# Block 2's mixers, emitted step by step between the K steps of its products

## The chip, the cores and the metric

One core of a Trainium2 chip runs the whole program in one launch. The metric is the device time of one execution in microseconds (us). The kernel before was timed three times.

## The reference

A sequence of 1024 tokens of width 1024 (float32) goes through two blocks of two layers each. Block 1 (`first_block`) is not touched by the change. A layer of block 2 (`second_block`) does, for the 1024 tokens `x` and, in its first layer only, for 256 context tokens as well:

```
hx = rmsnorm(x, g_pre_mix) * (1 + sc1) + sh1
q, k, v, u, gv, f = split(hx @ w_in)                  # 512, 128, 128, 256, 256, 256 columns
attn = latent_window_attention(rope(q), rope(k), v, ck, cv, sink)   # 8 heads, blocks of 128
sgu  = spatial_gating(gelu(u), gelu(gv), w_sgu, b_sgu, g_sgu)
four = fourier_mix(f)                                 # real part of a 2D FFT over tokens x 64
y = concat(rmsnorm(attn), rmsnorm(sgu), rmsnorm(four)) @ w_out
x = x + g1 * rmsnorm(y)
x = x + g2 * rmsnorm(square(relu(norm2(x) @ w_ff1)) @ w_ff2)        # inner width 4096
```

Attention of a block of 128 tokens sees the block before, itself and the block after, and the 256 context tokens (`ck`, `cv`); so a score row has 512 or 640 entries. The vectors sc1, sh1, g1 and so on come from two conditioning vectors times `w_ada`.

## The kernel before, in words

Tokens lie in eight blocks of 128 partitions, worked on in two groups of four (`GT` = 4). Every large product is done in a split form: each factor is a high and a low fp32r part, and an output takes three matmuls a K step (high x high, high x low, low x high).

`product` (line 463 and on) is the loop that all stages share. For each of its K steps it loads a weight tile of 128 x 512 (`wr`, SP's queue), splits it (`split_weights`: ACT makes `wh` at line 202, DVE makes `wl` at line 203; with gains the lines are 439 and 440), and issues three matmuls for each of up to four outputs (lines 502 and 506, banks `mm`). After each K step it calls `self.tick()`, which runs one step of the first generator in the list `self.bg`. Block 1 puts its mixers (attention, retention, gated linear attention) into this list as generators. Block 2 of the kernel before puts nothing there: its mixers are plain functions, and each is emitted as a whole between two products.

What stands first in the program need not run first. When the program is built, a planner fixes the order of the instructions on each engine: it plays the program through with durations that it estimates, and whenever an engine comes free it takes, of the instructions whose inputs and buffers are then ready, the one that was emitted first. `high_priority(n)` makes an instruction count as emitted n instructions earlier: weight splits 3000 (`HP`), evictions, `norm_T` and `merge` 800 (`HE`), `norm_x` 600 (`HX`). On the chip each engine keeps the order that the planner fixed. Buffers go by tags with a set number of places: PSUM has four `mm`, one `mt`, two `sm`, one `o`; SBUF among others four `x`, sixteen `H`, five `uv`, five `Z`, eight `pt`.

The parts of block 2:

- `norm_x` and `norm_T`: for four blocks `x`, sum of squares (ACT line 375), reciprocal root (POOL lines 208, 209), scaling in place (DVE line 377), then for each of eight K tiles four transposes into `mt` (PE line 398), scale and shift, split. `norm_T(lazy=True)` makes each K tile only when it is asked for.
- `s2_attn` (one block of tokens): `queries` for a pair of heads (POOL copy `qd` line 1357, PE transposes, ACT `qh` line 1361, DVE `qh` line 1362); `scores` of a head (PE line 1373 into `sm`, DVE lines 1375 and 1380, ACT exp line 1381); `values` of the head before (PE transposes line 524, ACT and DVE copies `pT` lines 1394 and 1392, PE line 1398 into `o`); a closing normalization.
- `s2_sgu`: four matmuls (line 1291) and DVE lines. `features` and `s2_four`: the Fourier transform; `four_out` does four matmuls (line 1328) into `sm`, then `section` (ACT sum of squares, POOL root), DVE scaling (line 1333), two transposes (line 524), for eight outputs, and `s2_four_ctx` for two more.
- `merge`: for each of six K tiles four transposes into `mt` (line 1432) and a split into `H` tiles; two more K tiles are split from the Fourier output. `merge_out` is the product with `w_out`, whose eviction `residual` adds the old `x`, and stores the new one (POOL's queue, line 579).
- `ff`: eight rounds, each a product of 8 K steps, an eviction (ACT line 1463, DVE line 1464, split), and two products of 4 K steps. `mix1`, merge and `merge_out` of the second group, is called in the last round of the first group's `ff`. `mods_acc` computes the next layer's conditioning vectors between the rounds.

In layer 1 block 2 starts with attention of blocks 0 to 2, and the products of the context follow; then the context's mixers, block 3, group 1's products, the context's merge, `s2_four`, group 0's merge, `norm_T`, the queries of group 1, attention of blocks 4 to 7, and `ff`. Layer 2 is the same without the context, and its `merge_out` of group 0 uses `product_rows` (line 462), which finishes one output after the other.

Of the kernel before, what the change touches and what calls it, by code (L numbers as in the profile page):

```python
# [162 lines left out]
class Net:  # L163
# [106 lines left out]
    def mods_acc(self, w, vecs, bias, mds, width, chunks):  # L270
# [6 lines left out]
        def close(ch, acc, nv):  # L277
# [986 lines left out]
    def features(self, f):  # L1264
# [3 lines left out]
        Z = []  # L1268
# [7 lines left out]
        return Z  # L1276
# [8 lines left out]
    def s2_sgu(self, l, ug):  # L1285
# [3 lines left out]
        for h in range(4):  # L1289
# [3 lines left out]
            nc.vector.scalar_tensor_tensor(uv, ps, bs[:, h:h + 1], uv, ALU.add, ALU.mult)  # L1293
        for t in range(nt):
# [3 lines left out]
    def s2_four(self, Z):  # L1298
# [9 lines left out]
        V.tensor_sub(A, A, Z2)  # L1308
        c, s = 0, 1
# [4 lines left out]
        f4 = [self.T("uv", [P, 2, 512]) for _ in range(2)]  # L1314
        for r, W in ((0, Z3), (2, A), (1, Z2), (3, Z0)):
            ft = self.T("x", [P, 2, 2, 256])
            self.load(ft, self.a["ftab"][r].rearrange("p (a b c) -> p a b c", a=2, b=2))
            for mt in range(2):
                self.four_out(ft, W, mt, f4[mt].rearrange("p k (m r) -> p k m r", r=4)[:, :, :, r])
        return f4  # L1320

    def four_out(self, ft, W, mt, dst):
        nc = self.nc
        ps = self.T("sm", [P, 256])
        n = 0
        for nt_ in range(2):
            for cs in range(2):
                nc.tensor.matmul(ps, lhsT=ft[:, nt_, cs, mt * P:(mt + 1) * P], rhs=W[:, nt_, cs, :],  # L1328
                                 start=n == 0, stop=n == 3)
                n += 1  # L1330
        rr = self.section(ps, 256, 1.0 / 256, EPS)
        y = self.T("sc", [P, 256])
        nc.vector.tensor_scalar(y, ps, rr, None, ALU.mult)
        self.transposes(dst, y, 2)

    def s2_four_ctx(self, Z):
        ft = self.T("x", [P, 2, 2, 256])
        self.load(ft, self.a["ftab"][4].rearrange("p (a b c) -> p a b c", a=2, b=2))
        f4 = self.T("uv", [P, 2, 256])
        for mt in range(2):  # L1340
            self.four_out(ft, Z[0], mt, f4[:, :, mt * P:(mt + 1) * P])
        return f4

    def s2_attn(self, l, q, parts):
# [3 lines left out]
        O = self.T("o", [P, 512])  # L1348
        m8 = self.T("ti", [P, 8])
        m8b = self.T("ti", [P, 8])  # L1350
        den = self.T("ti", [P, 8])
        nk = sum(n for (_, n, _, _) in parts)
        scs = {}

        def queries(c):
            d = self.T("qd", [P, 2, 2, 64])
            nc.gpsimd.tensor_copy(d, q[:, c * P:(c + 1) * P].rearrange("p (h d) -> p h d", d=64).unsqueeze(2)
                                  .to_broadcast([P, 2, 2, 64]))
            ps = self.transposes(None, d.rearrange("p h c d -> p (h c d)"), 2)
# [3 lines left out]
            return hi, lo  # L1363

        def scores(h, hl):
# [3 lines left out]
            for i, (K, n, mask, _) in enumerate(parts):  # L1369
                w = n * P  # L1370
# [11 lines left out]
            scs[h] = sc  # L1382

        def values(h):
            sl = slice(h // 4 * 64, h // 4 * 64 + 64)
            sc = scs.pop(h)
            pT = self.T("pT", [P, 5, P])
            for c0 in range(0, nk, 4):
                n = min(4, nk - c0)
                tp = self.transposes(None, sc[:, c0 * P:(c0 + n) * P], n)  # L1390
                if c0:
                    nc.vector.tensor_copy(pT[:, c0:c0 + n, :], tp)
                else:
                    nc.scalar.copy(pT[:, c0:c0 + n, :], tp)  # L1394
            i = 0
            for (_, n, _, Vs) in parts:
                for j in range(n):
# [4 lines left out]
        hl = queries(0)  # L1402
        for h in range(9):
            if h < 8:
                scores(h, hl)
            if h % 2 and h < 7:
                hl = queries(h // 2 + 1)
            if h:
                values(h - 1)
        es = self.T("ti", [P, 8])  # L1410
        nc.vector.tensor_tensor(es, sk, m8, ALU.subtract)
        nc.scalar.activation(es, es, AF.Exp)
        nc.vector.tensor_add(den, den, es)
        nc.vector.reciprocal(den, den)
        a = self.T("qa", [P, 512])
        nc.vector.tensor_tensor(a.rearrange("p (h d) -> p h d", d=64), O.rearrange("p (h d) -> p h d", d=64),
                                den.unsqueeze(2).to_broadcast([P, 8, 64]), ALU.mult)
        r = self.section(a, 512, 1.0 / 512, EPS)
        nc.vector.tensor_scalar(a, a, r, None, ALU.mult)
        return a  # L1420

    def merge(self, at, u2, f4):
# [4 lines left out]
        with self.tc.high_priority(self.HE):  # L1427
            for k in range(6):
# [5 lines left out]
            for k in (6, 7):  # L1434
                self.split(*get(k), f4[:, k - 6, :])
        return get, nt
# [77 lines left out]
    def block2(self, cur, n_layers, out, early=None, rest=None):  # L1514
        nc, a = self.nc, self.a
        with ExitStack() as ctx:
            self.open(ctx, "b2", {"uv": 5, "Z": 5, "k2": 1, "sc": 1, "p5": 2, "pT": 2, "ck2": 1, "qd": 1, "qh": 3, "tr": 1},
                      {"ac": "x", "aw": "x", "row": "x", "L": "M", "qa": "pt", "ys": "pt"})
# [13 lines left out]
            for l in range(n_layers):  # L1532
# [15 lines left out]
                def attn(tb, q):  # L1548
                    lo, hi = max(0, tb - 1), min(NB - 1, tb + 1)
                    n = hi - lo + 1  # L1550
                    m0 = (lo - tb + 1) * P
                    at[tb] = self.s2_attn(l, q, [(K[:, :, lo * P:(hi + 1) * P], n, band[:, m0:m0 + n * P],
                                                  lambda j: V[:, lo + j, :]), cpart])

                x1, x2 = self.stream(), self.stream()
                if last:
                    x2 = out
                if l == 0:
# [8 lines left out]
                    if rest:  # L1567
                        kept = rest(lambda: self.project(l, 512, 768, "A", hx, self.e2_kv(0, cK, cV, False)))
                        h1 = self.norm_T(self.norm_x(kept), first(mx, l))
# [3 lines left out]
                if l or not rest:  # L1573
                    self.project(l, 512, 768, "A", hx, self.e2_kv(0, cK, cV, False))
                if l == 0:
                    for tb in range(3):
                        attn(tb, q0[tb])
                        if tb == 0:
                            self.project(l, 768, 1280, "A", h0, ev)
                if not last:  # L1580
                    self.project(l, 0, 512, "A", hx, self.e2_q(0, False, qc))
                    self.project(l, 768, 1280, "A", hx, self.e2_ug(2, ugc))
                    self.project(l, 1280, 1536, "B", hx, self.e2_f(2, fc))
                if l == 0:
                    self.project(l, 1280, 1536, "B", h0, self.e2_f(GT, f0))
                    Z = self.features(f0)
                    self.s2_sgu(l, ug0)
# [142 lines left out]
```

## Time and profile before

| | us |
|---|---|
| median of three runs | 3931.77 |
| lowest and highest | 3928.83 and 3936.1 |
| the profiled execution | 3937.08 |
| its span | 3935.3 |
| TensorE's mean granted clock in it | 0.986 of full |

| engine | busy us | share of the span |
|---|---|---|
| PE (matmul) | 3726.1 | 95% |
| PEld (weight load) | 3045.4 | 77% |
| DVE | 2445.6 | 62% |
| ACT | 1685.8 | 43% |
| POOL | 649.3 | 17% |

PE, PEld, DVE, ACT, POOL are TensorE's matmuls, its weight loads (which overlap the matmuls), VectorE, ScalarE and GpSimd; SP is the engine that issues the loads. A busy PE counts from a matmul's start to its modelled end, so overlapping matmuls count once. "A <- B" after an idle time says that A's engine stood until B's instruction was done. In the trace the parts lie so: block 1 from 0 to about 1240 us; block 2, layer 1: mixers about 1240 to 1840, `ff` of group 0 to 2140 with `mix1` at its end, `ff` of group 1 and the context to 2760; layer 2: mixers about 2680 to 3220, `ff` of group 0 to 3600 with `mix1` from about 3470, `ff` of group 1 to the end.

### The profile page before, as it was taken

Reading aid. Unit: us, or ns where it says so; the run is one execution under the profiler, and the core shown is the slowest. Engines: PE = TensorE matmul, PEld = TensorE weight load, DVE = VectorE, ACT = ScalarE, POOL = GpSimd, SP = SyncE. Lnnn points to the kernel's source line nnn. Section 1 sums busy time; section 2 is a strip of 40 time slices with the busy share of each in tenths; the row PEclk is TensorE's granted clock in tenths of the full one; section 3 lists DMA queues with packets and bytes.
Section 4 is the critical chain, followed back from the end, with each engine's and each line's share of the span. In section 5 each row is a group of like instructions: output and inputs, shape, how many; then the busy total and the mean of one; then the engine's idle time right before and its main releaser. Section 6 shows DMA issues by size and latency. Waiting matters only on the chain. (4 is left out here: it accounts for less than half of the span.)

```text
span 3935.3 us, 55613 instructions
## 1 busy us (share of the span) xinstructions
PE 3726.1 (95%) x19144; PEld 3045.4 (77%) x19144; DVE 2445.6 (62%) x5209; ACT 1685.8 (43%) x3652; POOL 649.3 (17%) x1026
## 2 busy tenths in 40 slices
PE   7999999999999898899999999999899999999998
PEld 6877777877877787677887788888777788887886
DVE  7686787687687657576545643335765654455444
ACT  4443444454454555464334422224554543344333
POOL 2021134243252212131001000000311100001000
PEclk9999999999999999999999999999999999999999
DMA  6144344343343313333333632222412123334332
GB/s 213 50 134 121 113 143 121 109 129 110 105 136 98 103 56 107 108 108 105 126 102 110 209 110 68 62 66 89 145 54 86 69 64 97 97 100 166 97 97 94
DMA packets 249453, 420.37 MB, mean 107 GB/s; under 512 B 32002, under 2 KB 101203, under 8 KB 249171
## 3 DMA queue, kind: packets, MB, share of 16 engines
q1 hardware_dynamic: 241426, 389.52, 32.0%
q0 software_dynamic: 7744, 27.30, 1.9%
q8 instruction: 151, 2.47, 0.3%
q14 instruction: 132, 1.07, 0.1%
HBM read 389.42 MB, written 27.30 MB: 106 GB/s over the span
## 5 line engine op out<-in xcount | busy, mean ns | idle before, releaser
L203 DVE TENSOR_TENSOR wl<-wr,wh 128x512 fp32r<-128x512 f32 (+2 forms) x948 | 644.2, 682 | 812.9 <-ACT wh L202 809.4
L202 ACT CAST wh<-wr 128x512 fp32r<-128x512 f32 (+2 forms) x948 | 553.7, 585 | 1208.8 <-PE mm L502 489.8
L502 PE MATMUL mm<-wh,M 128*128 128x512 f32 (+1 forms) x2944 | 945.9, 393 | 24.6 <-ACT M L202 14.8
L502 PE MATMUL mm<-wh,H 128*128 128x512 f32 (+2 forms) x2432 | 791.5, 396 | 12.3 <-DVE pe L654 3.6
L506 PE MATMUL mm<-H,wh 128*128 128x512 f32 x2240 | 727.4, 395 | 1.8 <-ACT wh L202 1.7
L502 PEld LDWEIGHTS mm<-wh,M 128*128 128x128 f32 x2944 | 550.0, 190 | 142.8 <-ACT M L202 23.1
L502 PE MATMUL mm<-wl,M 128*128 128x512 f32 (+1 forms) x1472 | 576.0, 391 | 0.4 <-DVE wl L203 0.4
L502 PEld LDWEIGHTS mm<-wh,H 128*128 128x128 f32 x2432 | 450.0, 192 | 100.5 <-issue 4.7
L506 PEld LDWEIGHTS mm<-H,wh 128*128 128x128 f32 x2240 | 418.8, 189 | 82.2 <-ACT wh L202 2.0
L502 PE MATMUL mm<-wl,H 128*128 128x512 f32 (+2 forms) x1216 | 471.1, 388 | 0.0
L506 PE MATMUL mm<-H,wl 128*128 128x512 f32 x1120 | 444.5, 397 | 0.0
L502 PEld LDWEIGHTS mm<-wl,M 128*128 128x128 f32 x1472 | 279.8, 190 | 49.2 <-DVE wl L203 1.2
L502 PEld LDWEIGHTS mm<-wl,H 128*128 128x128 f32 x1216 | 234.0, 192 | 35.1 <-issue 0.2
L506 PEld LDWEIGHTS mm<-H,wl 128*128 128x128 f32 x1120 | 212.2, 189 | 37.2
L1398 PEld LDWEIGHTS o<-kv,pT 128*128 128x128 f32 x1280 | 158.1, 192 | 25.0 <-ACT pT L1394 20.4
L317 POOL TENSOR_TENSOR ac<-ac,aw 128x256 f32<-128x256 f32 x168 | 142.9, 851 | 162.8 <-ACT aw L316 143.9
L1398 PE MATMUL o<-kv,pT 128*128 128x64 f32 x1280 | 167.5, 274 | 1.6 <-ACT pT L1394 0.9
L311 DVE SCALAR_TENSOR_TENSOR ac<-aw,c,ac 128x256 f32<-128x256 f32 x280 | 160.1, 572 | 5.9 <-DMA aw<-in_w_ada 3.1
L1483 DVE TENSOR_TENSOR Z<-Z,mm 128x512 f32<-128x512 f32 x224 | 140.2, 681 | 2.8 <-PE mm L502 2.5
L558 POOL TENSOR_TENSOR tm<-tm 128x1 f32<-128x1 f32 x34 | 6.6, 196 | 763.3 <-ACT pe L553 762.9
L1375 DVE CUSTOM_DVE_ANT_0 p<-sm,c,c 128x384 f32<-128x384 f32 (+1 forms) x144 | 82.2, 571 | 76.0 <-PE sm L1373 74.5
L1381 ACT ACTIVATE p<-p,ti 128x640 f32<-128x640 f32 (+2 forms) x144 | 110.8, 770 | 43.1 <-DVE ti L1380 39.7
(353 smaller groups left out, 5703.1 us busy)
## 6 DMA issues: line engine op xcount, KB each, us to landing
wr<-in_w_ff SPq DMA_DIRECT2D x512, 256.0 KB, 2.7
wr<-in_w_in SPq DMA_DIRECT2D x240, 256.0 KB, 2.7
wr<-in_w_out SPq DMA_DIRECT2D x144, 256.0 KB, 2.7
x<-xd SPq DMA_DIRECT2D x64, 512.0 KB, 4.9
aw<-in_w_ada SPq DMA_DIRECT2D x192, 128.0 KB, 2.1
x<-in_w_ada SPq DMA_DIRECT2D x96, 256.0 KB, 2.9
xd<-x POOLq DMA_DIRECT2D x44, 512.0 KB, 3.8
wr<-in_w_in SPq DMA_DIRECT2D x152, 128.0 KB, 2.1
```

The source lines that it names most:

```text
L202: self.nc.scalar.copy(hi, src)
L203: self.nc.vector.tensor_sub(lo, src, hi.bitcast(F32))
L311: nc.vector.scalar_tensor_tensor(acc[:, 0], wt, c[0], acc[:, 0], ALU.mult, ALU.add)
L317: nc.gpsimd.tensor_tensor(acc[:, 1], acc[:, 1], wt, ALU.add)
L502: nc.tensor.matmul(acc[j][:, :ncol], lhsT=x[:, j * P:(j + 1) * P], rhs=y[:, :ncol], start=first, stop=last)
L506: nc.tensor.matmul(acc[j][:m, :w], lhsT=y[:, j * P:j * P + m], rhs=x[:, :w], start=first, stop=last)
L558: nc.gpsimd.tensor_tensor(ss[j][:, 0:1], ss[j][:, 0:1], ss[j][:, 1:2], ALU.add)
L1375: nc.vector.tensor_tensor_reduce(sc[:, at:at + w], ps[:, :w], mask, 1.0, prev, ALU.add, ALU.max, accum_out=acc)
L1381: nc.scalar.activation(sc[:, :at], sc[:, :at], AF.Exp, bias=nm, accum_out=den[:, h:h + 1])
L1398: nc.tensor.matmul(O[:, h * 64:h * 64 + 64], lhsT=pT[:, i, :], rhs=Vs(j)[:, sl], start=i == 0, stop=i == nk - 1)
L1483: nc.vector.tensor_add(y, y, ps)
```

## The change

The mixers of block 2 become generators with a `yield` after each step, and are put on `self.bg`, so that `tick` emits one step after each K step of the products. In `s2_attn` one generator now does several blocks in a row; a step is one head's scores, the values of the head before, the transposes for the pair of heads that comes next, and the POOL copy for the pair after that. `four_out` becomes `four_outs`: the transposes of an output are emitted one step later, after the next output's matmuls, and the output is first copied out of PSUM by ACT. `norm_steps` emits one K tile of `norm_T` a step. `merge` loses its `high_priority`. `until(g)` ticks until g is done, `drain()` until the list is empty. The accumulators `ac` of `mods_acc` lie in `uv` places in block 2, not in `x` places, and their transposes go to `mt`, not to `o`. Layer 2's `merge_out` of group 0 uses `product` like the others, and attention of blocks 4 to 7 is on the list during it and during the `norm_T` that follows; in layer 1 it is on the list during `ff`. Some stages change places, as the diff of `block2` shows.

```
-                    ps = self.T("o", [P, each, nb, P])
+                    ps = self.T("mt", [P, each, nb, P])
...
+    def until(self, work):
+        while work in self.bg:
+            self.tick()
...
+    def four_outs(self, outs):
+        ft, have, pend = None, None, None
+        for r, W, mt, dst in outs + [(None,) * 4]:
+            y = None
+            if W is not None:
...
+                for n in range(4):
+                    nc.tensor.matmul(ps, lhsT=ft[:, n // 2, n % 2, mt * P:(mt + 1) * P], rhs=W[:, n // 2, n % 2, :],
+                                     start=n == 0, stop=n == 3)
+                y = self.T("pe", [P, 512])[:, :256]
+                nc.scalar.copy(y, ps)
+                rr = self.section(y, 256, 1.0 / 256, EPS)
+                nc.vector.tensor_scalar(y, y, rr, None, ALU.mult)
+            if pend:
+                self.transposes(pend[1], pend[0], 2)
+            pend = (y, dst)
+            yield True
...
+        units = [(n, h) for n in range(len(jobs)) for h in range(8)]
+        copies(0, 0)
+        yield True
+        queries(0, 0)
+        for i in range(len(units) + 1):
+            if i < len(units):
+                scores(*units[i])
+            if i:
+                n, h = units[i - 1]
+                values(n, h)
+                if h == 7:
+                    close(n)
+            if i + 2 < len(units):
+                (n, h), two = units[i + 1], units[i + 2]
+                if h % 2 == 0:
+                    queries(n, h // 2)
+                if two[1] % 2 == 0:
+                    copies(two[0], two[1] // 2)
+            yield True
...
-        with self.tc.high_priority(self.HE):
-            for k in range(6):
+        for k in range(8):
+            if k < 6:
                 ps = self.T("mt", [P, nt, P])
...
+                yield True
...
+    def norm_steps(self, xs, ab, room, keep):
+        ready, nt = self.norm_T(xs, ab, room=room, lazy=True)
+        keep += [ready, nt]
+        for k in range(8):
+            ready(k)
+            yield True
...
-                      {"ac": "x", "aw": "x", "row": "x", "L": "M", "qa": "pt", "ys": "pt"})
+                      {"ac": "uv", "aw": "x", "row": "x", "L": "M", "qa": "pt", "ys": "pt"})
...
+                    bg.append(attn((0,), q0))
+                    made = self.norm_steps(self.norm_x(kept), first(mx, l), "L", h1)
+                    bg += [made, attn((1, 2), q0[1:])]
+                    self.project(l, 768, 1280, "A", h0, ev)
+                    self.project(l, 0, 512, "A", hx, self.e2_q(0, False, qc))
+                    self.project(l, 768, 1280, "A", hx, self.e2_ug(2, ugc))
+                    self.project(l, 1280, 1536, "B", hx, self.e2_f(2, fc))
+                    bg.append(self.s2_sgu(l, ug0))
+                    bg.append(self.s2_attn(l, [(qc[t], [cpart], lambda a, t=t: atc.__setitem__(t, a)) for t in range(2)]))
+                    self.project(l, 1280, 1536, "B", h0, self.e2_f(GT, f0))
+                    bg.append(self.s2_features(fc, Zc))
+                    bg.append(self.s2_sgu(l, ugc))
                 else:
...
+                    made = self.norm_steps(self.norm_x(cur[4:8]), first(mx, l), "L", h1)
+                    bg += [attn((0, 1, 2), q0), made, self.s2_sgu(l, ug0)]
+                    self.project(l, 1280, 1536, "B", h0, self.e2_f(GT, f0))
+                bg.append(self.s2_features(f0, Z))
+                self.until(made)
+                self.project(l, 512, 768, "A", h1, self.e2_kv(4, K, V, True))
+                bg.append(attn((3,), q0[3:]))
+                self.project(l, 1280, 1536, "B", h1, self.e2_f(GT, f1))
+                bg.append(self.s2_features(f1, Z))
                 if not last:
+                    bg.append(self.s2_four_ctx(Zc, f4c))
                 self.project(l, 768, 1280, "A", h1, self.e2_ug(GT, ug1))
                 if not last:
...
+                    self.drain()
+                    for _ in self.merge(atc, ugc[0], f4c[0], mTc):
+                        pass
+                    bg.append(self.s2_four(Z, f4))
+                    self.merge_out(l, mTc, self.row_of(mc, 16), hc, c1)
+                    bg.append(self.s2_sgu(l, ug1))
+                    self.drain()
+                else:
+                    bg.append(self.s2_four(Z, f4))
+                    bg.append(self.s2_sgu(l, ug1))
+                    self.project(l, 0, 512, "A", h1, self.e2_q(4, True, q1))
+                    self.drain()
+                for _ in self.merge(at[:4], ug0[0], f4[0], mT0):
+                    pass
                 if last:
+                    bg.append(attn(range(4, 8), q1))
+                kept = self.merge_out(l, mT0, self.row_of(mx, 16, "Z"), cur[0:4], x1[0:4])
+                abf = second(mx, l)
+                if last:
+                    ready = self.norm_T(self.norm_x(kept), abf, room="H", lazy=True)
+                    for k in range(8):
+                        ready[0](k)
+                        for _ in range(2):
+                            self.tick()
+                    hT = ready
+                else:
+                    bg.append(self.norm_steps(self.norm_x(kept), abf, "H", hT))
                     self.project(l, 0, 512, "A", h1, self.e2_q(4, True, q1))
+                    self.drain()
+                    bg.append(attn(range(4, 8), q1))
...
                 def mix1():
-                    mT = self.merge(at[4:], ug1[0], f4[1])
+                    self.drain()
+                    for _ in self.merge(at[4:], ug1[0], f4[1], mT1):
+                        pass
```

## Rows read from the trace of the kernel before

**Rows 1.** The page's first part: busy us (share of the span) xinstructions.

```profile
PE 3726.1 (95%) x19144; PEld 3045.4 (77%) x19144; DVE 2445.6 (62%) x5209; ACT 1685.8 (43%) x3652; POOL 649.3 (17%) x1026
```

**Rows 2.** Windows: length, busy PE PEld DVE ACT POOL (instructions), PEclk, DMA share, GB/s.

```profile
100.00:1240.00 1140.00, 1077.33 (x5782) 870.55 (x5780) 880.65 (x1956) 530.32 (x1302) 345.76 (x492) 0.99 0.37 113
1240.00:1840.00 600.00, 558.50 (x3117) 453.16 (x3117) 385.57 (x976) 316.52 (x711) 129.10 (x215) 0.97 0.31 96
1880.00:2140.00 260.00, 259.57 (x1151) 212.23 (x1150) 127.27 (x197) 90.45 (x158) 4.69 (x10) 1.00 0.33 104
2680.00:3220.00 540.00, 504.63 (x2869) 412.53 (x2868) 336.49 (x890) 273.45 (x621) 90.70 (x183) 0.97 0.26 85
3220.00:3520.00 300.00, 299.92 (x1327) 245.18 (x1326) 146.15 (x225) 105.83 (x181) 0.00 (x0) 1.00 0.31 96
```

**Rows 3.** The same view in shorter windows of the mixers.

```profile
1320.00:1340.00 20.00, 14.83 (x56) 11.56 (x55) 14.92 (x33) 10.15 (x21) 7.97 (x12) 0.85 0.40 118
...
1520.00:1560.00 40.00, 33.02 (x139) 25.56 (x138) 30.61 (x60) 24.19 (x53) 14.94 (x27) 0.91 0.33 106
...
1620.00:1665.00 45.00, 36.81 (x155) 27.87 (x154) 32.39 (x65) 21.60 (x40) 14.73 (x26) 0.89 0.39 129
1665.00:1835.00 170.00, 165.70 (x990) 132.93 (x989) 118.48 (x311) 97.72 (x202) 39.34 (x44) 1.00 0.27 86
...
3060.00:3080.00 20.00, 15.51 (x78) 11.89 (x77) 12.73 (x32) 11.90 (x25) 8.10 (x15) 0.74 0.13 53
3080.00:3220.00 140.00, 139.37 (x862) 113.69 (x860) 76.02 (x238) 73.49 (x162) 8.15 (x21) 1.00 0.18 60
```

**Rows 4.** Who PE waited for, 1240 to 1880 us: total, times, longest.

```profile
PE mt L398 <- DVE x L377: 7.3, 5, 2.9
PE sm L524 <- DVE sc L1333: 5.6, 9, 0.8
PE sm L1373 <- ACT qh L1361: 4.1, 2, 2.8
PE sm L524 <- POOL qd L1357: 3.9, 1, 3.9
PE sm L1291 <- POOL uv L1249: 2.7, 1, 2.7
...
PE sm L524 <- DVE ti L1375: 2.6, 6, 1.2
PE sm L1373 <- DVE qh L1362: 2.4, 1, 2.4
PE mt L1432 <- DVE H L203: 2.3, 2, 1.4
```

**Rows 5.** The same, 2680 to 3230 us.

```profile
PE mt L398 <- DVE x L377: 9.8, 4, 4.9
...
PE sm L524 <- DVE sc L1333: 4.5, 7, 1.5
...
PE sm L1373 <- ACT qh L1361: 2.9, 2, 2.1
...
PE sm L524 <- DVE ti L1375: 1.1, 3, 0.5
```

**Rows 6.** Timeline, layer 1, normalization after group 0's merge: start, us, engine, instruction [idle before].

```profile
1639.42 0.75 DVE L377 TENSOR_SCALAR x<-x,tm 128x1024 f32<-128x1024 f32 x1 [2.93 <-DMA xd<-x]
```

**Rows 7.** Timeline, layer 1, Fourier outputs.

```profile
1579.06 0.48 DVE L1333 TENSOR_SCALAR sc<-sm,ti 128x256 f32<-128x256 f32 x1 [3.67 <-POOL ti L209]
```

**Rows 8.** Timeline, layer 1, merge of group 1, in the last feed-forward round.

```profile
2070.49 0.59 ACT L202 CAST H<-mt 128x512 fp32r<-128x512 f32 x1 [1.87 <-PE mm L506]
...
2071.88 0.64 PE L1432 MATMUL mt<-c,pt 128*128 128x128 f32 x4
```

**Rows 9.** Groups by line, 1880 to 2140 us: busy, mean ns, idle before.

```profile
L203 DVE TENSOR_TENSOR M<-pe,M 128x512 fp32r<-128x512 f32 x20 | 13.4, 690 | 2.9 <-ACT M L202 2.7
...
L1463 ACT ACTIVATE pe<-mm 128x512 f32<-128x512 f32 x20 | 11.8, 594 | 0.6
```

More of the change, by code (lines that the diff above doesn't have):

```diff
@@ L1320, in s2_four @@
-        return f4
-    def four_out(self, ft, W, mt, dst):
-        nc = self.nc
[L1324 to L1344, printed above, removed]
+                outs.append((r, W, mt, f4[mt].rearrange("p k (m r) -> p k m r", r=4)[:, :, :, r]))
+        yield from self.four_outs(outs)
+    def s2_four_ctx(self, Z, f4):
+        f4 += [self.T("uv", [P, 2, 256])]
+        yield from self.four_outs([(4, Z[0], mt, f4[0][:, :, mt * P:(mt + 1) * P]) for mt in range(2)])
@@ L1346, in s2_attn, with copies @@
+    def s2_attn(self, l, jobs):
         nc = self.nc
         sk = self.rows[:, 16 + l * 8:16 + l * 8 + 8]
[L1348 to L1357, printed above, removed]
+        scs, hls, work, qds = {}, {}, {}, {}
+        def copies(n, c):
+            d = qds[n, c] = self.T("qd", [P, 2, 2, 64])
+            nc.gpsimd.tensor_copy(d, jobs[n][0][:, c * P:(c + 1) * P].rearrange("p (h d) -> p h d", d=64).unsqueeze(2)
@@ L1400, in values, with close, merge @@
                     i += 1
[L1402 to L1422, printed above, removed]
+        def close(n):
+            O, m8, _, den = work.pop(n)
+            es = self.T("ti", [P, 8])
+            nc.vector.tensor_tensor(es, sk, m8, ALU.subtract)
+            nc.scalar.activation(es, es, AF.Exp)
+            nc.vector.tensor_add(den, den, es)
+            nc.vector.reciprocal(den, den)
+            a = self.T("qa", [P, 512])
+            nc.vector.tensor_tensor(a.rearrange("p (h d) -> p h d", d=64), O.rearrange("p (h d) -> p h d", d=64),
+                                    den.unsqueeze(2).to_broadcast([P, 8, 64]), ALU.mult)
+            r = self.section(a, 512, 1.0 / 512, EPS)
+            nc.vector.tensor_scalar(a, a, r, None, ALU.mult)
+            jobs[n][2](a)
+        units = [(n, h) for n in range(len(jobs)) for h in range(8)]
+        copies(0, 0)
+        yield True
+        queries(0, 0)
[13 more added lines that the diff above has]
+                    copies(two[0], two[1] // 2)
+            yield True
+    def merge(self, at, u2, f4, keep):
         nc = self.nc
@@ L1584, in block2 @@
[L1584 to L1587, printed above, removed]
-                if l or not rest:
-                    h1 = self.norm_T(self.norm_x(cur[4:8]), first(mx, l))
-                if not last:
-                    Zc = self.features(fc)
-                    self.s2_sgu(l, ugc)
-                    f4c = self.s2_four_ctx(Zc)
-                    atc = [self.s2_attn(l, qc[t], [cpart]) for t in range(2)]
@@ L1615, in block2 @@
-                kept = self.merge_out(l, mT, self.row_of(mx, 16, "Z"), cur[0:4], x1[0:4], "M" if last else None)
-                abf = second(mx, l)
-                hT = self.norm_T(self.norm_x(kept), abf, room="H")
-                if not last:
-                    self.project(l, 0, 512, "A", h1, self.e2_q(4, True, q1))
-                for tb in range(4, 8):
-                    attn(tb, q1[tb - 4])
+                    self.drain()
+                    for _ in self.merge(atc, ugc[0], f4c[0], mTc):
+                        pass
```

109 lines of the change are left out of this document (51 added, 58 removed).

## The prediction

> **What bounds the kernel now.** I began with the page's busy table: PE is busy for 95% of the span [rows 1]. A gain can only come from the rest, or from PE time at the lower clock. Next came the view by windows, cut at the stages [rows 2]. The reader is to see two kinds of stretch. In the feed-forward PE is busy for 259.6 of 260 us and 299.9 of 300 at a granted clock of 1.00: nothing is to be had there. In the two stretches with the mixers PE is idle for 600 − 558.5 = 41.5 and 540 − 504.6 = 35.4 us, and the clock is 0.97: 0.03 x 1140 = 34 us of work lost at the lower of its two levels (a mean clock c over w us costs w(1 − c)). So about 111 us lie in the stretches that the change rewrites; that is the whole purse.
>
> Then the short windows [rows 3]. They show that the purse is not where the attention is. The second group's attention already lies within the feed-forward: the planner filled its waits with feed-forward matmuls, though they are emitted later, and PE is busy for 165.7 of 170 us in layer 1 and 139.4 of 140 in layer 2, at clock 1.00. The idle time stands at seams: 1320 to 1340, 1520 to 1560, 1620 to 1665, 3060 to 3080, with clocks of 0.85, 0.91, 0.89 and 0.74. Last I read who PE waited for there [rows 4, 5]. The longest are normalization (DVE line 377), Fourier outputs (line 1333), and the first queries of an attention block (lines 1361, 1362, 1357).
>
> **The change part by part.** The matmuls and their shapes stay the same, so each term is a wait. All are set against the profiled execution (3937.08, span 3935.3), which is 5.3 us above the median; I move the difference to the median.
>
> *Attention in layer 1's feed-forward.* 32 heads in 170 us are 5.3 us a head; a K step is twelve matmuls at 260/1151 us, 2.7 us [rows 2, 3]. So one head a K step is about the pace that the planner found by itself. At most 4.3 us of idle are left there and 0.6 in layer 2 [rows 3]. They are not a term of their own: they lie in the attention's waits below.
>
> *Fourier outputs.* Today two transposes wait for sum of squares, root and scaling of the very output whose matmuls just ran [rows 7]: 5.6 and 4.5 us [rows 4, 5]. After, the next output's matmuls and a K step of the product stand between. Bounds: −10.1 and 0. I take −9, as the K step (2.7 us, half in the context's product) is longer than the longest of these waits (1.5). The ten added ACT copies cost at most 10 x 0.59 us [rows 8], on an engine busy for 317 of 600 us [rows 2]; PE's matmuls hide them, and without that cover they are +6.
>
> *Attention's own waits.* Queries 4.1 + 3.9 + 2.4 + 2.9, running maxima 2.6 + 1.1: 17.0 us [rows 4, 5]. The POOL copy is now emitted two steps ahead of its use, the query transposes one. This also joins blocks, so the cold starts fall from ten to five in layer 1, from eight to three in layer 2. Product matmuls of the same step no longer rank behind the whole attention, which gives DVE and ACT slack against a planner that thinks them faster than they are. Bounds: −17, and +5 should each remaining start wait longer, as the attention also no longer outranks the products on PE. I take −10, nearest to the query waits.
>
> *Clock at these seams.* 20 x 0.15 = 3.0 us at 1320 and 40 x 0.09 = 3.6 at 1520 go with their waits; of 45 x 0.11 = 5.0 at 1620 I count the share of the query wait, 1 [rows 3]. Bounds −12 and 0; taken −6. *Spatial gating* (2.7, [rows 4]) is emitted later, well after its eviction: −2, between −2.7 and 0.
>
> *Normalization* waits 7.3 and 9.8 us [rows 4, 5] are mostly out of reach. DVE scales `x` in place and must wait for the store of the same `x` to land, 2.93 us [rows 6], with weight splits queued behind it; `norm_x` and `norm_T` keep their head starts of 600 and 800 instructions, so PE's transposes come in the same place. POOL's stores and SP's loads pass nothing new: DMA is at a share of 0.26 to 0.31 in these stretches [rows 2], and no wait of [rows 4, 5] is a load. One place changes: after layer 2's merge sixteen attention steps are emitted between the K tiles, where PE now stands 4.5 us and loses 20 x 0.26 = 5.2 to the clock [rows 3]. Against this stands that `product` ends its four outputs together, where `product_rows` ended them one by one, so the chain to the first K tile grows. Bounds −9.7 and +6 (two more waits as in [rows 6]); taken −5.
>
> *Merges without head start.* Now the second group's merge goes into PE's queue between K steps of the last round, as `H` tiles come free: its transposes start at 2071.9, 1.4 us after the cast of the tile before them, long before that product's end [rows 8]. After, they rank behind all of that product's matmuls. Then PE meets one K tile's chain uncovered, 0.64 + 0.59 + 0.69 = 1.9 us, and on ACT the casts queue behind the eviction of four outputs, up to 4 x (0.595 + 0.59) = 4.7 us [rows 8, 9]. Part of that eviction runs before the product ends, and the next product can fill. Bounds: 0 and 6.6 for each of the two layers' last rounds, taken 3 each: +6. The three other merges follow a `drain`, so they have attention or Fourier work beside them, and already wait 2.3 [rows 4]: +2, between −2 and +8. `ac` in `uv` and its transposes in `mt`: nothing on the path, as five places hold the four tiles in use and this one; ±2.
>
> Sum: −9 −10 −6 −2 −5 +6 +2 = −24 us: 3937 to 3913 for the profiled execution, 3931.8 to **3908 us** for the median.
>
> **A cross-check from block 1**, whose mixers already run by ticks: PE is busy for 94.5% there at clock 0.99, against 93.1% and 93.5% at 0.97 [rows 2]. At its level the mixers would save 600 x (1 − 0.931/0.945) + 540 x (1 − 0.935/0.945) = 9 + 6 us of idle and 0.02 x 1140 = 23 of clock, 38 in all. My sum is inside that.
>
> **The rivals.** (1) *All seams close.* The mixers reach the feed-forward's density. Read from weight loads: 0.816 and 0.817 of the time there, 0.755 and 0.764 in the mixers [rows 2], so 600 x (1 − 0.755/0.816) + 540 x (1 − 0.764/0.817) = 45 + 35 = 80 us: 3852; three quarters of it, 3872, is nearer. For it: same instructions, more cover. Against: block 1 with ticks has 0.764 as well, and the normalizations stay. The Trainium skill ("Perfetto Trace Analysis", section "Identifying the Most-Contended Engine") says that matmul busy share is no good measure of headroom and weight-load share is. By that page this reading, 80 us to be had but only 6.5 if block 1's level is all that ticks reach, weighs more than my cross-check of 38; the trace here shows both shares low in the same windows and so does not decide.
>
> (2) *Nothing moves.* The planner already fills by readiness, and boosts of evictions, splits and normalization are as before; waits change names. By weight loads block 1's level is worth 600 x (1 − 0.755/0.764) = 7 us: 3925, or anywhere within 8 of 3932. For it: 1665 to 1835 and 3080 to 3220 [rows 3] came out dense unaided.
>
> (3) *Slower: merges without head start.* Each of the five merges may stand with its full chain, six K tiles through one `mt` bank, 6 x 1.9 = 11.4, behind 4.7 of eviction: 16 us at worst [rows 8, 9]. The rest of my sum is −32, so from 32/5 = 6.4 us a merge the change is slower. At 10 us each it is −32 + 50 = +18: 3950. For it: the present merges cost PE almost nothing in the last round [rows 2], and all of that is given up. Against: only the first K tile must precede the first K step, as a K step (2.7) is longer than a tile's chain.
>
> **How the numbers follow.** Forecast 0.52 (own range 3885 to 3924), rival 1 0.10, rival 2 0.17, rival 3 0.21. Two runs of this kernel tell a difference from about 0.2%, 8 us. Faster is forecast and rival 1, 0.62; same is rival 2, 0.17; slower is rival 3, 0.21. The range 3868 to 3946 leaves out about 0.05 below and 0.13 above: the more complete closings of rival 1, and merges at 9 us and more.
>
> **What would show it.** Right: waits of line 524 on the Fourier scaling nearly gone; waits on query tiles halved; the window after layer 2's merge at a clock near 1.0; waits on line 377 still there before both normalizations; two new waits of about 3 us where `mix1` begins; mixer stretches at 94 to 95% busy. Wrong: idle time that only moved to the drains; merges of 7 us or more; or a normalization that lost its waits, which would make the gain larger.

## The result, and the profile after

The kernel after takes 3969.98 us (median of four runs, 3963.12 to 3974.19), the kernel before 3933.93 on the same chip (four runs): a ratio of 1.0091, 95% interval 1.0071 to 1.011, so 0.9% slower. The prediction, 3908 and a range up to 3946, was wrong in sign and in range. The profiled execution took 3971.8 us with a span of 3970.0 and a mean granted clock of 0.980.

The page's first part, columns as in [rows 1]:

```profile
PE 3747.9 (94%) x19144; PEld 3057.4 (77%) x19144; DVE 2443.8 (62%) x5209; ACT 1697.7 (43%) x3670; POOL 654.7 (16%) x1026
```

The matmul count is the same. The view by windows, columns as in [rows 2]; after 1600 us everything lies some 30 us later, so the windows of layer 2 are moved by 31:

```profile
100.00:1240.00 1140.00, 1077.24 (x5765) 872.81 (x5765) 875.55 (x1943) 526.96 (x1291) 346.56 (x491) 0.99 0.37 113
1240.00:1870.00 630.00, 580.67 (x3133) 465.47 (x3132) 385.26 (x978) 324.85 (x730) 127.77 (x211) 0.95 0.29 92
1910.00:2170.00 260.00, 258.49 (x1144) 210.63 (x1143) 128.96 (x199) 90.37 (x157) 4.32 (x10) 1.00 0.34 107
2711.00:3255.00 544.00, 508.22 (x2883) 414.49 (x2883) 337.40 (x893) 280.65 (x633) 92.52 (x183) 0.97 0.26 85
```

Layer 1's mixers are 30 us longer; layer 2's, 540 us before, 4 longer; the feed-forward and block 1 are as before. Following one event through both traces gives the same: the store of group 0's merged `x` in layer 1 is 27.7 us later than before, the start of layer 2 31.0, the end 34.7. Shorter windows, first two of the kernel before (new ones, so they are shown), then after:

```profile
1320.00:1480.00 160.00, 149.85 (x920) 125.21 (x919) 102.86 (x322) 87.68 (x236) 32.05 (x66) 0.98 0.22 63
1480.00:1560.00 80.00, 71.57 (x379) 57.45 (x378) 59.57 (x132) 43.40 (x94) 17.88 (x29) 0.96 0.26 83
```

```profile
1320.00:1480.00 160.00, 154.72 (x974) 128.97 (x974) 102.80 (x323) 96.12 (x244) 27.35 (x56) 1.00 0.25 76
...
1520.00:1540.00 20.00, 16.93 (x67) 13.89 (x66) 5.69 (x23) 4.98 (x12) 0.00 (x0) 0.50 0.01 1
...
1480.00:1560.00 80.00, 60.63 (x252) 46.09 (x250) 40.69 (x105) 26.44 (x58) 15.25 (x25) 0.74 0.06 20
...
3120.00:3140.00 20.00, 10.85 (x61) 8.38 (x60) 13.77 (x29) 10.70 (x24) 12.32 (x23) 0.82 0.35 131
```

From 1320 to 1480 the steps do what they were meant to: 4.9 us less idle and a clock of 1.00 for 0.98, 3.2 us. Then 1480 to 1560 loses 19.4 us idle and 0.26 x 80 = 20.8 to the clock, against 8.4 and 3.2 before: 28.6 us more, the size of the 30 that layer 1 lost in all. (With the 8.1 us won just before, some 10 us more must have gone in other stretches of layer 1; they are not traced here.) From 1520 to 1540 DVE is busy for 5.69 us, POOL for none and DMA at 0.01: no engine was overworked. What PE stood for, 1475 to 1565 us (columns as in [rows 4]):

```profile
PE mt L1277 <- DVE Z L1278: 6.9, 5, 3.7
PE sm L528 <- DVE ti L1389: 2.6, 6, 0.6
PE mt L1465 <- DVE H L203: 2.3, 1, 2.3
PE sm L1387 <- ACT qh L1370: 2.0, 3, 1.1
```

These four name 13.8 of 19.4 us, the smaller ones most of the rest; the slow clock, and why no product ran, stand in no wait. The timeline shows it (start, us, engine, line, [idle before]): the features of group 1 and the context's Fourier outputs.

```profile
1502.77 0.68 DVE L1278 COPY Z<-mt 128x512 f32<-128x512 f32 x1
1504.65 0.60 PE L1277 MATMUL mt<-c,Z 128*128 128x256 f32 x2
1543.26 4.43 PE L1344 MATMUL sm<-Z,x 128*128 128x256 f32 x14
1548.17 0.69 DVE L1278 COPY Z<-mt 128x512 f32<-128x512 f32 x1
1548.91 1.13 PE L1277 MATMUL mt<-c,Z 128*128 128x256 f32 x4 [0.16 <-DVE Z L1278]
1550.78 0.68 DVE L1278 COPY Z<-mt 128x512 f32<-128x512 f32 x1
1551.52 0.44 PE L1465 MATMUL mt<-c,pt 128*128 128x128 f32 x2 [0.16 <-DVE Z L1278]
```

Group 1's third block of features is in `mt` at 1505.3, but its copy starts at 1548.2, 43 us later. It opens a new `Z` tile, and five are taken: two of group 0's features, the transposed features of group 1, its first `Z` tile, and the context's, which is released only by the context's Fourier outputs (line 1344). These were put on the list *behind* attention of block 3 and ran at 1540 to 1547.7. So the one `mt` bank was held from 1504.7 to 1548, and what needs it, the context's merge (line 1465, from 1551.5), could not begin. The gating product had ended at 1484.2, and the next product's matmul started at 1552.4; from 1505 to 1540 PE ran block 3's attention, a chain, and nothing else. The Trainium skill ("Perfetto Trace Analysis", section "Optimization Strategy") says that consistent bubbles, the same gap repeating on the engine that should be saturated, can mean that there isn't enough SBUF or PSUM for the next tile. This trace has the cause but not that form: no repeated gap, but one copy of 0.69 us that stood for 43.

The other prediction lines: PE's waits in layer 1 (1240 to 1880) and, behind the dots, layer 2 (2680 to 3260), beside [rows 4, 5]:

```profile
PE mt L398 <- DVE x L377: 6.8, 5, 2.7
PE sm L528 <- DVE ti L1389: 4.7, 12, 0.8
PE sm L1387 <- ACT qh L1370: 3.9, 5, 1.4
PE sm L528 <- POOL qd L1364: 3.7, 1, 3.7
...
PE sm L528 <- DVE pe L1349: 2.2, 3, 0.9
...
PE mt L398 <- DVE x L377: 14.5, 4, 7.8
...
PE sm L528 <- DVE pe L1349: 2.2, 3, 1.0
PE sm L1387 <- ACT qh L1370: 2.1, 1, 2.1
```

The Fourier scaling (line 1349) costs 4.4 us where it cost 10.1; query waits and running maxima are about as they were; the normalization in layer 2 waits 14.5 for 9.8, all of the difference after the merge (7.8 for 3.1 there, 6.7 ahead of it in both).

### The profile page after: what moved, and what is told of

Same layout as the page of the kernel before. It is cut to its first block, busy times and chain, and to the rows that moved or that the text cites. A ratio compares the mean times of both kernels' runs of the same rounds, so it can differ in the third digit from the quotient of the medians.

```text
span 3970.0 us, 55608 instructions
## 1 busy us (share of the span) xinstructions
PE 3747.9 (94%) x19144; PEld 3057.4 (77%) x19144; DVE 2443.8 (62%) x5209; ACT 1697.7 (43%) x3670; POOL 654.7 (16%) x1026
## 5 line engine op out<-in xcount | busy, mean ns | idle before, releaser
L506 PE MATMUL mm<-wh,H 128*128 128x512 f32 (+2 forms) x2496 | 821.5, 396 | 13.9 <-DVE pe L658 3.6
L506 PEld LDWEIGHTS mm<-wh,H 128*128 128x128 f32 x2496 | 461.9, 193 | 104.3 <-ACT H L202 6.0
L506 PE MATMUL mm<-wl,H 128*128 128x512 f32 (+2 forms) x1248 | 484.6, 388 | 0.0
L1412 ACT COPY pT<-sm 128x512 f32<-128x512 f32 (+1 forms) x144 | 80.6, 560 | 141.2 <-PE sm L528 140.3
```

Of the source, the lines that this page charges most:

```text
L506: nc.tensor.matmul(acc[j][:, :ncol], lhsT=x[:, j * P:(j + 1) * P], rhs=y[:, :ncol], start=first, stop=last)
L1412: nc.scalar.copy(pT[:, c0:c0 + nb, :], tp)
```

## The experiments

Theory A: layer 1 loses by the missing `Z` place. Theory B: it loses because the list is emptied with no product beside it, whatever lies in it. Each ratio is to the kernel before on the same chip (medians 3936.55 to 3937.9 there).

**The context's Fourier outputs ahead of group 1's features** (and of block 3's attention), the rest as after:

```
                     bg.append(self.s2_sgu(l, ug0))
...
                     bg.append(self.s2_sgu(l, ugc))
+                    bg.append(self.s2_four_ctx(Zc, f4c))
...
-                if not last:
-                    bg.append(self.s2_four_ctx(Zc, f4c))
```

> The changed kernel, with the context's Fourier outputs put on the list right after the context's spatial gating, ahead of block 3's attention and of group 1's features. Theory A, a missing place: group 1's features need a sixth Z tile (five are there), get it only when the context's Fourier outputs have read theirs, and those stood behind all of block 3's attention; meanwhile the one mt bank holds a finished feature tile, so the context's merge and its product cannot start and TensorE has nothing but one attention chain. Then the stretch with a clock of 0.74 goes: idle time in the 80 us after the gating-input product of group 1 falls from 19 to under 8 us, the clock there rises to 0.95 or more, and the time falls by 20 to 32 us, to 3938 to 3950. Theory B, the drain itself: block 3's attention is emitted after the last product, so it stands alone whatever the buffers do: idle stays above 14 us there and the time falls by less than 10 us.

Measured 3951.89, ratio 1.0036 (1.0023 to 1.0048). From 1480 to 1560 PE is busy for 68.39 us at clock 0.91. That is between the theories' marks: 11.6 us idle (under 8 and over 14 were named), and a gain of 22 us by the ratios, theory A's size, with the time 2 us above its range. This edit changes the order and frees the place at once, so it doesn't tell the two apart.

**A sixth place**: group 1's transposed features lie in two `H` tiles in layer 1, the order as after:

```
-                self.project(l, 1280, 1536, "B", h1, self.e2_f(GT, f1))
+                self.project(l, 1280, 1536, "B", h1, self.e2_f(GT, f1, "Z" if last else "H"))
```

> The changed kernel in its own order, with group 1's transposed features in two H tiles (free at that point) in layer 1, so that five Z places are enough. Theory A (a missing place): 15 to 32 us faster than the changed kernel, near the kernel with the context's Fourier outputs first, though these still stand behind block 3's attention. Theory B (the drain itself): within 8 us of the changed kernel. If it is the rank of the context's Fourier outputs behind the attention that matters, since the merge needs them, and not the place: between the two, 5 to 15 us faster.

Measured 3944.48, ratio 1.0018 (1.0007 to 1.0028). Its features' copies (the view of tile `Z`, first and last start) and the window:

```profile
L1282 DVE COPY Z<-mt x4: 681/690/692, 1496.6 to 1506.1; 128x512 f32<-128x512 f32 x4
...
1480.00:1560.00 80.00, 68.80 (x358) 54.46 (x358) 54.28 (x130) 40.26 (x90) 19.14 (x26) 0.94 0.23 73
```

The last copy is at 1506.1, not 1550.8. A place alone, with no change of order, gives back 0.0073 x 3935 = 29 of the 36 us, as theory A said; the context's outputs still stand behind block 3's attention here, so it is not their rank that cost this. Undoing the order alone gives 22.

**The reverse, in the kernel before**: only the context's Fourier outputs moved, behind group 1's gating product and its spatial gating. No list, no steps.

```
-                    f4c = self.s2_four_ctx(Zc)
                     atc = [self.s2_attn(l, qc[t], [cpart]) for t in range(2)]
...
+                    f4c = self.s2_four_ctx(Zc)
                     mT = self.merge(atc, ugc[0], f4c)
```

> The kernel before, with one thing of the change alone: the context's Fourier outputs, which free the fifth Z place, are emitted after group 1's gating product, not before the context's attention. No list, no steps, no drain. Theory A (the missing place by itself stops the mt bank, whatever the emission): features of group 1 wait for the place, the time rises by 8 to 30 us, 3946 to 3968 (ratio 1.002 to 1.008). Theory B (the missing place hurts only where the list is drained with no product beside it; here the planner fills with the gating product and the later ones): within 5 us of before, 3933 to 3943.

Measured 3959.39, ratio 1.0054 (1.004 to 1.0068): 21 us, in theory A's range. A hole in the same window:

```profile
1480.00:1560.00 80.00, 55.63 (x259) 41.87 (x258) 42.73 (x92) 27.86 (x63) 15.74 (x27) 0.81 0.13 42
...
1539.93 0.69 DVE L1275 COPY Z<-mt 128x512 f32<-128x512 f32 x1 [3.37 <-PE sm L1328]
...
PE sm L1291 <- POOL uv L1249: 16.4, 1, 16.4
```

The third block of features was in `mt` at 1471 and was copied at 1539.9, after the context's Fourier outputs (line 1328): the bank was held for 69 us. Until 1510 PE had the gating product and attention beside it. Then it stood 16.4 us in one piece (last line, a wait of 2.7 us before [rows 4]) for group 1's spatial gating, behind which the context's outputs now lie. So the hole has another face: one long wait, and not attention alone at a low clock. The move by itself costs 21 us without list or steps; whether by the place, or because the context's merge itself gets its Fourier outputs later, this run can't tell, and no run gives this kernel a sixth place.

The sixth place in the kernel after does tell: theory A holds there for the bulk, 29 of 36 us.

**Layer 2's rows form back** in the kernel after, so that the merge's outputs end one by one again:

```
-                kept = self.merge_out(l, mT0, self.row_of(mx, 16, "Z"), cur[0:4], x1[0:4])
+                kept = self.merge_out(l, mT0, self.row_of(mx, 16, "Z"), cur[0:4], x1[0:4], "M" if last else None)
```

> The changed kernel, with layer 2's merge product of group 0 finishing one output after the other again. If the wait of 7.8 us of the first normalized transposes there comes from four outputs that end together, it falls to 3 to 4 us, and the time by 4 to 9 us, to 3961 to 3966. If it comes from the head start that puts those transposes ahead of attention in TensorE's order, the wait stays above 6 us and the time within 4 us of the changed kernel; it may rise by some us, as eight K steps lose their attention steps.

Measured 3972.62, ratio 1.0088 (1.0072 to 1.0104): no difference that shows. The normalization after the merge waits 3.1 us in three pieces (longest 1.5) for 7.8 in one, and its profiled execution gains some 2 us in layer 2's mixers; in the medians nothing is left of it. So the wait came from the four outputs that end together, as the first reading had it, but it was not worth the 4 to 9 us.

**The Fourier lag alone** in the kernel before (`four_out` replaced by `four_outs`, nothing else):

> The kernel before, with one part of the change alone: each Fourier output is copied out of PSUM and its transposes are emitted after the next output's matmuls. My prediction had 9 us for this; from the waits of the changed kernel (2.2 and 2.2 us left of 5.6 and 4.5) it is 5.7. So 3926 to 3930; if the planner had filled these waits anyway, 3932 to 3936.

Measured 3933.65, ratio 0.9989 (0.998 to 0.9997): −4 us (−8 to −1) against 3937.9 on the same chip, with 3.0 + 1.8 us left on the scaling, line 1343 there, against 5.6 + 4.5.

**Features ahead**, with the sixth place; each step of `s2_features` gets a head start of 800 instructions. 12 us were still idle or slow between 1480 and 1500, where the copies stand in DVE's order behind the gating product's eviction.

```
+            with self.tc.high_priority(self.HE):
```

> The sixth place of the earlier run, and each step of the features (two matmuls into mt, DVE's copy) counts as emitted 800 instructions earlier. Theory A (what is left between 1480 and 1500, some 12 us, is DVE: the features' copies stand behind the eviction of the gating product, and with one mt bank each copy holds the next matmuls): the waits of L1281 on the Z copy fall from 6.7 to under 3 us, the window 1480 to 1560 gains 6 to 12 us of PE, and the time is 3934 to 3940 (ratio 0.999 to 1.0005). Theory B (attention of block 3 runs out of product matmuls to stand beside, whoever comes first): the idle time passes to other waits, 3943 to 3947 (ratio 1.0015 to 1.0025).

Measured 3955.38, ratio 1.0043 (1.0031 to 1.0056): worse than either theory said. The feature waits are gone, and attention's chain (first and last line; the middle one, the normalization, is 3.2 in the run with the place alone) stands instead, 1470 to 1660 us:

```profile
PE sm L1392 <- DVE ti L1394: 4.2, 2, 2.6
PE mt L398 <- DVE x L377: 3.4, 4, 2.5
PE sm L1392 <- DVE qh L1376: 2.1, 1, 2.1
```

From 1480 to 1560 PE is busy for 66.48 us at 0.87, against 68.80 at 0.94 with the place alone. A reading that fits, not tested by itself: where attention is all that PE has, features put ahead of it on DVE lengthen the only chain.

**Attention of blocks 4 to 7 whole**, with the sixth place: emitted ahead of `ff` in both layers, in layer 2 after the normalization.

```
-                if last:
-                    bg.append(attn(range(4, 8), q1))
                 kept = self.merge_out(...)
...
+                    bg.append(attn(range(4, 8), q1))
+                    self.drain()
```

> The sixth place, and attention of blocks 4 to 7 is emitted whole ahead of the feed-forward in both layers, as in the kernel before; in layer 2 after the normalization, not in it. If attention step by step within the feed-forward costs what the earlier run lost in layer 2 (5.8 us in the mixers) and in layer 1's feed-forward (2.5 us), the time falls from 3944.5 to 3936 to 3940 (ratio 0.9995 to 1.0005). If the planner makes the same order of both, as the dense windows of before suggested, it stays at 3942 to 3947. The prediction's own step (attention step by step saves waits) would make it slower, 3948 or more.

Measured 3945.26, ratio 1.0018 (1.0008 to 1.0028): the same as with the steps. Emitting the second group's attention step by step within the feed-forward is worth nothing here; the planner put it there unasked.

**The merges' head start back**, with the sixth place; in `merge`, around its K tiles:

```
+        with self.tc.high_priority(self.HE):
```

> The sixth place, and the merges have their head start of 800 instructions back. By the prediction's third rival and its terms of 6 and 2 us for the merges the time falls by 4 to 8 us, 3936 to 3940. By what the trace shows at the start of mix1 (1.4 us of lost PE time in each layer) it falls by no more than 3 us: 3941 to 3946 (ratio 1.001 to 1.002). Slower than 3947 if the merge's transposes, once ahead, take the mt bank from the features.

Measured 3938.89, ratio 1.0003 (0.9994 to 1.0012): some 6 us less than without (the two intervals overlap). Group 1's first merge transposes start at 2075.2 for 2089.2.

**The head start taken from the kernel before**, nothing else:

> The kernel before, with the merges' head start of 800 instructions taken away and nothing else. By the prediction's terms (3 us where each mix1 begins, some 2 us for the other merges) it is 4 to 10 us slower, 3940 to 3947 (ratio 1.001 to 1.0025); giving the head start back in the list form was worth about 6. If the loss belongs to the list form alone (merges behind a drain), the kernel before stays within 2 us, 3935 to 3939. Rival 3 as written (10 us a merge) would make it 3975 or more.

Measured 3959.78, ratio 1.0056 (1.0044 to 1.0068): 22 us, above both terms and below rival 3 as written. Of 22.7 us between the two profiled executions 8.1 lie in layer 2's mixers, 4.8 between layer 1's context store and group 0's, and 4.3 ahead of the context's store, whose merge lost its head start too. Where the merge's transposes (line 1432) and the Fourier outputs (line 1328) run in layer 2, first and last start, and 60 us around them: the kernel before, then this one, which is 12 us late by then:

```profile
L1432 PE MATMUL mt<-c,pt x13: 271/273/330, 2986.0 to 2994.1; 128*128 128x128 f32 x13
...
L1328 PE MATMUL sm<-Z,x x64: 378/379/382, 2995.6 to 3033.5; 128*128 128x256 f32 x64
...
2980.00:3040.00 60.00, 53.81 (x257) 42.26 (x256) 35.76 (x80) 29.49 (x67) 10.84 (x27) 1.00 0.35 114
```

```profile
L1432 PE MATMUL mt<-c,pt x13: 272/272/273, 3006.9 to 3027.8; 128*128 128x128 f32 x13
...
L1328 PE MATMUL sm<-Z,x x64: 377/379/631, 3005.2 to 3043.9; 128*128 128x256 f32 x64
...
2992.00:3052.00 60.00, 50.54 (x240) 38.61 (x240) 30.95 (x79) 25.18 (x59) 11.16 (x27) 0.94 0.24 72
```

With its head start the merge is done with attention's tiles before the Fourier outputs begin, and the `w_out` product stands beside these. Without it the tiles are made between the outputs, the product comes later, and the outputs stand more alone: 3.3 us more idle and 0.06 x 60 = 3.6 of clock. In the list form the same line runs from 3003.4 to 3023.2 without the head start and from 2991.9 to 2999.8 with it. The rest of the 22 us, some 5 at the ends of both `ff`, stays open.

**The context's merge first**: sixth place, head start, rows form, and in layer 1 the context's merge and its output product ahead of the gating product (`fx` is the generator of the context's Fourier outputs):

```
                 bg.append(self.s2_features(f1, Z))
+                self.until(fx)
+                for _ in self.merge(atc, ugc[0], f4c[0], mTc):
+                    pass
+                bg.append(self.s2_four(Z, f4))
+                self.merge_out(l, mTc, self.row_of(mc, 16), hc, c1)
                 self.project(l, 768, 1280, "A", h1, self.e2_ug(GT, ug1))
```

> The change with the sixth place, the merges' head start and layer 2's rows form, and in layer 1 another order: the context's Fourier outputs, its merge and its output product come before the gating product of group 1, so that attention of block 3 has three products beside it in place of two, and group 1's gating waits for mix1. Theory A (the drain is short of products; 12 us lost at 1480 to 1500): PE is busy for 74 us or more of each 80 us from 1400 to 1640, and the time falls to 3922 to 3932 (ratio 0.9965 to 0.999). Theory B (the loss goes where the list is drained, whatever is drained): 3934 to 3941 (ratio 0.9995 to 1.001).

Measured 3944.13, ratio 1.0015 (1.0003 to 1.0026): above both theories' ranges, and 9 us slower than the same without this order (0.9992, next run). Its profiled execution, 3933.93, was 10 us faster than its median, so the windows show where the idle time went but not the whole loss. The hole closed and another opened 40 us earlier, at the `until`, where no product runs beside attention and the context's outputs:

```profile
1440.00:1480.00 40.00, 35.65 (x158) 27.17 (x158) 17.74 (x64) 18.34 (x60) 5.33 (x14) 0.70 0.00 1
1480.00:1560.00 80.00, 77.31 (x426) 62.02 (x425) 53.68 (x118) 42.55 (x100) 15.16 (x29) 1.00 0.39 124
```

These 40 us lose 4.4 idle and 12.0 to the clock, about what 1480 to 1560 loses without this order (10.9 and 7.2). For what is left once the place is there this speaks for theory B: the loss goes where the list is emptied.

**Rows and head start**, with the sixth place, in the order of the kernel after:

> The same without the other order in layer 1: sixth place, merges' head start, and layer 2's output product ends one output after the other again. Against the run with the head start (ratio 1.0003) only the rows form differs. With attention step by step within the feed-forward the earlier run found it worth nothing: 3937 to 3941. If the last normalization is what layer 2 still loses (about 2 us in its mixers): 3932 to 3937 (ratio 0.999 to 1.0).

Measured 3935.83, ratio 0.9992 (0.9983 to 1.0001).

**Layer 2 whole**: the same, and each generator of layer 2 followed at once by `self.drain()`, in the order of before:

> As the one with sixth place, head start and rows, and layer 2's mixers are emitted whole again, each drained as soon as it is listed, in the order of the kernel before. If the step form costs in layer 2 (segments of the earlier runs: 2 to 6 us more than before from the start of layer 2 to its mix1), this one is 2 to 5 us faster than the one before it in this group: 3932 to 3936. If the planner's order is as good either way: within 2 us of it.

Measured 3930.74, ratio 0.9985 (0.9976 to 0.9993): some 6 us faster than before, and the fastest here; the lag alone (0.9989) lies within its interval. The steps of layer 2 are worth nothing, or cost up to a few us.

The ladder, each rung with the ones before: after 1.0091, a place 1.0018, the head start 1.0003, the rows 0.9992, layer 2 whole 0.9985. The first rung is 29 of the 42 us between the ends; of the others no single one is outside the intervals, only two or more together.

## Why the prediction was wrong

**The step that failed is "Fourier outputs"**, with its bounds "−10.1 and 0". It priced the lag inside `four_outs` and not the move of the context's outputs behind group 1's features and attention of block 3, which the diff shows plainly. A late reader keeps a place: that term was +29 us (a place given to the kernel after), and the same kind of move put into the kernel before cost 21. The prediction did count places for `uv` ("five places hold the four tiles in use and this one") and not for `Z`, five places as well, and for no tag did it ask which bank is held meanwhile. The range's upper end came from the merges; no rival named a place. The list of what would prove it wrong did name the form, "idle time that only moved to the drains".

**The lag itself** (−9) was right in its mechanism and about half the size: −4 alone, between −8 and −1. Waits on the scaling went from 10.1 to 4.4 us, not to nearly none.

**Attention's own waits** (−10) did not come as written. Query and maxima waits in layer 1 are 13.9 us with the steps (line 1371 with 1.6 counted), 13.0 before: the 3.7 us cold start on POOL's copy is there as before. What did come is the stretch 1320 to 1480, 8 us with its clock, with products standing between the steps. It was given back at 1480 to 1560, where attention outlasts the products; with the place restored that window still loses 11.2 us idle and 4.8 to the clock, 4.4 more than before.

**Clock** (−6): the seam at 1320 closed, that at 1520 became the hole. **Spatial gating** (−2) came: its 2.7 us wait on POOL is gone. **Layer 2's normalization** (−5) was a loss of about 5 in its waits, and its own counter-argument won: the four outputs ending together put 7.8 us of PE's wait into one piece, 3.1 before, while the attention steps emitted between K tiles did not fill it: in the window 3120 to 3140 above PE is idle for 9.2 us and loses 3.6 to the clock, where the prediction had 4.5 and 5.2 to win back. The rows form removes the piece, but on its own not the time.

**Merges without head start** (+6 and +2): giving the head start back was worth about 6 in the list form, so the size was near. Rival 3 was real in sign, and 22 us in the kernel before, but its place was mostly another: not the chain of K tiles at `mix1` (in the kernel after PE waits nowhere for line 1465 in the last `ff` round), but the context's and group 0's merges. The prediction took it that these "have attention or Fourier work beside them"; in layer 2 it is the Fourier outputs that need the merge's product beside them, and so the merge ahead.

**Attention in `ff`** as no term of its own was right: whole or in steps, the same time. **`ac` in `uv`** (±2) was tested by no run; over the whole span PE waits 11.7 us for the transposes of `mods_acc` (line 294) where it waited 5.2, so the term may be larger, and the ladder's last rung still pays it. **The cross-check** from block 1 was too low for the stretch it fits best: from 1320 to 1480 weight loads reach 128.97/160 = 0.806, above block 1's 0.764 and near the feed-forward's 0.816. But it was 0.783 there before, so the steps gave 0.023. Rival 1's density is nearly reached where products stand beside attention; at the seams, where none is left, it was not to be had.

## What to carry to other kernels

When work is moved behind other work, list each tile that it reads and ask what will wait for that place, and which bank or engine that waiter holds meanwhile: a wait for room shows up as another tile's idle time. In these runs work emitted in steps paid while product steps stood beside it, and the gain was paid back where the list was emptied with no product left. Before rewriting the emission, test one place more and one move alone; here they decided more than the whole rewrite.

## What was not expected of the hardware

PE can be busy and slow at once: from 1520 to 1540 of the kernel after it was busy for 16.93 of 20 us, with attention alone, at a granted clock of 0.50, the lower of its two levels (1.2 GHz) throughout, after 40 us in which it had been busy for 28.5. In the kernel with the context's merge first 1460 to 1480 was busy for 18.71 us at 0.54, while the seam 1320 to 1340 of the kernel before, busy for 14.83, had 0.85 [rows 3]. Busy share alone does not tell the clock, and the low clock itself raises it: ten matmuls of 128x64 (line 1416, line 1398 before) take 2.23 us in this stretch, and 1.22 in the kernel before at 1510, where the clock was 1.00. Half the price of the hole was this.
